# Feed-forward output product in pairs of column blocks, with seven block products for eight in 7 of 11 chunks

## The chip, the cores and the metric

The kernel runs on one core of a Trainium2 chip. The metric is the device time of one execution in microseconds (us). Before the change three executions took 1455.44, 1457.18 and 1457.25 us; the median is 1457.18 us.

The engines are named as in the profile: PE is TensorE (matrix products), PEld its weight load, DVE VectorE, ACT ScalarE, POOL GpSimd, SP SyncE, which issues the loads.

## The reference, cut to what matters

The layer takes `x` (256 tokens x 2048), runs two mixers with an output projection, adds the result to `x`, and then runs a gated feed-forward part:

```
h = rms_norm(x, norm_ffn)
gate_up = h @ w_ffn_in                    # (256 x 2048) @ (2048 x 11264)
ff_gate, ff_up = split(gate_up)           # each 256 x 5632
x = x + (silu(ff_gate) * ff_up) @ w_ffn_out    # (256 x 5632) @ (5632 x 2048)
```

Everything is float32. The change lies in the last line, the feed-forward output.

## The kernel before, in words

**Products.** All large products go through one function, `product` (L137). It makes 256 tokens times 512 columns of a weight. The tokens are two halves `m` of 128; the weight's rows are cut into k-tiles of 128, and four k-tiles by 512 columns are one chunk (1 MB). A float32 value is held as a high and a low part in the type float32r, and each block product is three matmuls: high x high (L152), high x low part of the weight (L153), low part of the activation x high (L154). A matmul takes a 128x128 piece of the activations as stationary operand and 512 columns of the weight as the moving one. So a chunk is 4 k-tiles x 2 halves x 3 = 24 matmuls. The feed-forward output has 11 chunks for each of 4 column blocks: 4 x 11 x 24 = 1056 matmuls, which accumulate into two PSUM banks per column block.

**Weights.** `fetch` (L112) loads a chunk on SP's queue into one of 4 buffers `raw`. `load_weights` (L121) cuts it in two halves of two k-tiles; for each, ACT writes the high part `whi` (a cast, L131) and DVE the low part `wlo` (raw minus high, L132), both 128x1024. There are 4 buffers of `whi` and 4 of `wlo`, so a cast has to wait until PE has finished with the half chunk four places earlier. A raw buffer is free when DVE has made the second low part from it.

**Activations.** In the feed-forward input (L646 on), every column block `j` of 512 hidden channels ends as `hn` (tokens x channels); PE transposes it in two pairs of k-tiles while the next products run, and ACT and DVE split it into `hT` high and low (L178, L179). These pieces are generators that move on by a step at every `tick`, half a chunk of products.

**Order.** A scheduler fixes the order of each engine's instructions at build time by priority; the preparation of weights has a priority some 500 instructions ahead of the products. On the chip every engine runs its own list in order and waits by semaphores.

**End.** After the 11 chunks of a column block DVE adds the two banks to the residual `xs` (L672) and SP stores them.

Of the kernel before, what the change touches and what calls it, by code (L numbers as in the profile page):

```python
# [10 lines left out]
F32 = mybir.dt.float32  # L11
# [6 lines left out]
P = 128  # L18
# [10 lines left out]
# columns of the packed per-partition parameters  # L29
# [4 lines left out]
N_WARM = 5  # L34


@with_exitstack
def block_kernel(ctx: ExitStack, tc: tile.TileContext, x, x_t, w_in, w_pa, w_pb, w_out, w_fi, w_fo,
# [11 lines left out]
    aux = ctx.enter_context(tc.tile_pool(name="aux", bufs=4, space=bass.MemoryType.PSUM))  # L50

# [21 lines left out]
    # ---------------------------------------------------------------- constants  # L73
# [7 lines left out]
    # products of zeros, so that TensorE's clock is up when the first weights are there  # L81
# [27 lines left out]
    # ---------------------------------------------------------------- weights  # L109
# [11 lines left out]
    def load_weights(w, nb, kc, n=2, raw=None):  # L121
        """One chunk of 4 k-tiles x 512 columns as high and low float32r halves."""
# [14 lines left out]
    def product(w, nb, n_chunks, act, prologue=None, last=False):  # L137
        """act^T (k x 256 tokens, high and low parts) times 512 columns of w."""
# [20 lines left out]

    def split_tiles(s):  # L160
# [12 lines left out]
    def transpose_split_pair(nat, pair, hi, lo, gain=None):  # L173
        """Transposed high and low parts of half of nat, times a gain per channel if given."""
        pt = transpose_pair(nat, pair)
        if gain is None:
# [4 lines left out]
            return  # L181
# [8 lines left out]
    def transpose_split(nat, hi, lo, gain=None, wait=2):  # L190
        for _ in range(wait):
            yield 1
        for pair in range(2):
            transpose_split_pair(nat, pair, hi, lo, gain)
            yield 1

# [6 lines left out]
    # ---------------------------------------------------------------- x: load, norm, transpose  # L203
# [18 lines left out]
    def x_block(c):  # L222
        """Loads of x^T and of the first weights in the order of their use, then of x itself."""
# [33 lines left out]
    # ---------------------------------------------------------------- constants of the mixers  # L257
# [6 lines left out]
    # lower bound: softmax over the two rows of logits, first row  # L264
# [21 lines left out]
    # ---------------------------------------------------------------- HGRN2, 4 heads at a time  # L286
# [15 lines left out]
    def hgrn_forget(ps, half, b, kk):  # L302
        """Cumulative log decay within 64 tokens, and k = 1 - f; [channel, head, token]."""
# [50 lines left out]
    def parts(L):  # L354
        """For each of the first three of 4 runs of L tokens: that run, columns of the later ones."""
# [57 lines left out]
    def next_factors(b, qT):  # L413
        """The queries as they are, then those of odd tokens decayed by one step."""
# [9 lines left out]
    def next_scores(kk, eq, acc):  # L424
        """Scores of each token with itself (zero elsewhere) and of odd tokens with the previous."""
# [67 lines left out]
    # ---------------------------------------------------------------- attention, 4 heads at a time  # L493
# [23 lines left out]
    def attention(half, pair, qT, kT, v, yh, yl):  # L517
# [3 lines left out]
        # a query of the first chunk of a tile does not see the tile's second chunk  # L521
# [96 lines left out]
    # ---------------------------------------------------------------- branch projections, merge  # L618
# [14 lines left out]
    # ---------------------------------------------------------------- output projection, residual  # L633
# [14 lines left out]
    # ---------------------------------------------------------------- SwiGLU  # L648
    act_x2 = picker(x2T)
    hT = []  # L650
    for j in range(NJ):
# [9 lines left out]
        start(transpose_split(hn, *hT[j]))  # L661
# [3 lines left out]
    for nb in range(4):  # L665
        ps = product(w_fo, nb, NJ, act_h, last=nb == 3)
        for m in range(2):
            pieces = 2 if nb == 3 and m == 1 else 1
            w = 512 // pieces
            for i in range(pieces):  # L670
                sl = slice(i * w, (i + 1) * w)
                nc.vector.tensor_tensor(out=xs[nb][:, m, sl], in0=ps[m][:, sl],  # L672
                                        in1=xs[nb][:, m, sl], op=ALU.add)
# [65 lines left out]
```

## Time and profile before

| | us |
|---|---|
| span of the profiled execution (first to last instruction) | 1454.8 |
| executions timed without a profile | 1455.44, 1457.18, 1457.25 |
| median of these, less the span | 2.4 |
| PE busy | 1446.9 (99%) |
| DVE busy | 805.1 (55%) |
| ACT busy | 685.9 (47%) |
| POOL busy | 36.5 (3%) |
| DMA engines, share of the span | 54.4% |

The profiled execution's own time is known by its span alone; the 2.4 us beside it are what lies around the span, and the spread of the executions. A matmul's row shows some 389 ns although the next one starts 0.227 us after it: matmuls are pipelined, so a sum over rows is not the time they take, and the start of the first and of the last have to be compared. "Idle before" in a row is the time for which the engine stood still before that group, with what ended it.

### The profile page before, as it was taken

What the parts mean: (1) busy time and instruction counts of PE and PEld (TensorE: products, weight loads), DVE (VectorE), ACT (ScalarE), POOL (GpSimd) and SP (SyncE); (2) the same over time, 40 slices, a digit from 0 to 9 for tenths busy, and PEclk for the clock granted to TensorE, in tenths of its full rate; (3) what the DMA queues carried; (4) which work ended last, traced back from release to release, by engine and by line L of the source; (5) the groups of instructions that cost most, each with busy time, mean ns of one, the idle gap of its engine ahead of it and who ended that gap; (6) DMA issues with size and microseconds to landing.
All of it is one profiled execution on the core that took longest, in us unless ns stands there. A gap on an engine that the chain in (4) does not pass through costs nothing.

```text
span 1454.8 us, 16455 instructions
## 1 busy us (share of the span) xinstructions
PE 1446.9 (99%) x6586; PEld 1201.6 (83%) x6586; DVE 805.1 (55%) x910; ACT 685.9 (47%) x869; POOL 36.5 (3%) x37
## 2 busy tenths in 40 slices
PE   8999999999999999999999999999999999999998
PEld 6888888888888888888888888888888888888887
DVE  6768868564554555655545555545554455444443
ACT  6756655555544444445444444444444444334332
POOL 0100100100000000100000000000000000000000
PEclk9999999999999999999999999999999999999999
DMA  9554354446555555555555555555555555655561
GB/s 361 211 201 163 129 191 155 173 156 215 183 203 198 207 193 183 194 182 178 198 178 199 177 199 185 191 184 192 187 189 198 179 197 179 207 199 204 199 208 52
DMA packets 42635, 275.68 MB, mean 189 GB/s; under 512 B 4800, under 2 KB 5056, under 8 KB 10816
## 3 DMA queue, kind: packets, MB, share of 16 engines
q1 hardware_dynamic: 42560, 274.64, 54.4%
q8 instruction: 51, 0.84, 0.2%
q14 instruction: 24, 0.20, 0.0%
HBM read 272.53 MB, written 2.10 MB: 189 GB/s over the span
## 4 chain that ended last, share of the span: by engine, by line
PE 99%; DMA 1%; SPq 0%; ACT 0%; issue 0%; DVE 0%; DVEq 0%
PE mm L152 31%; PE mm L153 31%; PE mm L154 31%; PE bank L169 2%; PE bank L400 1%; DMA xt<-in_x_t 1%; PE bank L430 0%; PE bank L476 0%; PE bank L527 0%; PE bank L555 0%; PE bank L565 0%; PE bank L474 0%; PE bank L567 0%; PE bank L463 0%; PE bank L563 0%; PE bank L529 0%
## 5 line engine op out<-in xcount | busy, mean ns | idle before, releaser
L132 DVE TENSOR_TENSOR wlo<-raw,whi 128x1024 fp32r<-128x1024 f32 (+1 forms) x508 | 618.6, 1220 | 595.0 <-ACT whi L131 594.8
L131 ACT CAST whi<-raw 128x1024 fp32r<-128x1024 f32 (+1 forms) x508 | 530.4, 1046 | 693.2 <-PE mm L154 670.8
L152 PE MATMUL mm<-whi,xTh 128*128 128x512 f32 x704 | 276.2, 397 | 2.8 <-ACT whi L131 2.8
L152 PE MATMUL mm<-whi,x2Th 128*128 128x512 f32 x704 | 276.3, 393 | 0.0
L154 PE MATMUL mm<-whi,xTl 128*128 128x512 f32 x704 | 274.9, 391 | 0.0
L153 PE MATMUL mm<-wlo,xTh 128*128 128x512 f32 x704 | 274.7, 390 | 0.0
L154 PE MATMUL mm<-whi,x2Tl 128*128 128x512 f32 x704 | 274.2, 390 | 0.0
L153 PE MATMUL mm<-wlo,x2Th 128*128 128x512 f32 x704 | 274.2, 389 | 0.0
L152 PEld LDWEIGHTS mm<-whi,xTh 128*128 128x128 f32 x704 | 132.1, 188 | 29.7 <-ACT whi L131 3.9
L154 PEld LDWEIGHTS mm<-whi,x2Tl 128*128 128x128 f32 x704 | 132.2, 188 | 28.1
L154 PEld LDWEIGHTS mm<-whi,xTl 128*128 128x128 f32 x704 | 132.2, 188 | 27.8
L153 PEld LDWEIGHTS mm<-wlo,x2Th 128*128 128x128 f32 x704 | 132.3, 188 | 26.9
L153 PEld LDWEIGHTS mm<-wlo,xTh 128*128 128x128 f32 x704 | 132.3, 188 | 26.7 <-DVE wlo L132 0.9
L152 PEld LDWEIGHTS mm<-whi,x2Th 128*128 128x128 f32 x704 | 132.2, 188 | 26.7
L152 PE MATMUL mm<-whi,hTh 128*128 128x512 f32 x352 | 137.2, 390 | 0.0
L153 PE MATMUL mm<-wlo,hTh 128*128 128x512 f32 x352 | 137.0, 389 | 0.0
L154 PE MATMUL mm<-whi,hTl 128*128 128x512 f32 x352 | 137.0, 389 | 0.0
L154 PEld LDWEIGHTS mm<-whi,hTl 128*128 128x128 f32 x352 | 66.1, 188 | 13.8
L152 PEld LDWEIGHTS mm<-whi,hTh 128*128 128x128 f32 x352 | 66.1, 188 | 13.8
L153 PEld LDWEIGHTS mm<-wlo,hTh 128*128 128x128 f32 x352 | 66.1, 188 | 13.5
L152 PE MATMUL mm<-whi,mTh 128*128 128x512 f32 x128 | 50.7, 396 | 0.0
L154 PE MATMUL mm<-whi,mTl 128*128 128x512 f32 x128 | 49.9, 390 | 0.0
(171 smaller groups left out, 947.0 us busy)
## 6 DMA issues: line engine op xcount, KB each, us to landing
raw<-in_w_fi SPq DMA_DIRECT2D x88, 1024.0 KB, 4.8
raw<-in_w_in SPq DMA_DIRECT2D x84, 1024.0 KB, 4.8
raw<-in_w_fo SPq DMA_DIRECT2D x44, 1024.0 KB, 4.7
raw<-in_w_out SPq DMA_DIRECT2D x16, 1024.0 KB, 4.8
raw<-in_w_pa SPq DMA_DIRECT2D x8, 1024.0 KB, 5.0
raw<-in_w_pb SPq DMA_DIRECT2D x8, 1024.0 KB, 4.8
raw<-in_w_in SPq DMA_DIRECT2D x8, 256.0 KB, 7.4
raw<-in_w_in SPq DMA_DIRECT2D x4, 512.0 KB, 8.3
```

What stands on the lines that cost most here:

```text
L131: nc.scalar.copy(hi[:, sl, :], src[:, sl, :])
L132: nc.vector.tensor_tensor(out=lo[:, sl, :], in0=src[:, sl, :], in1=hi[:, sl, :].bitcast(F32), op=ALU.subtract)
L152: nc.tensor.matmul(ps[m], lhsT=ah, rhs=wh, start=kc == 0 and k4 == 0, stop=False)
L153: nc.tensor.matmul(ps[m], lhsT=ah, rhs=wl, start=False, stop=False)
L154: nc.tensor.matmul(ps[m], lhsT=al, rhs=wh, start=False, stop=kc == n_chunks - 1 and k4 == 3)
L169: nc.tensor.transpose(out=pt[:, j, m * P:(m + 1) * P], in_=nat[:, m, c:c + P], identity=ident)
L400: nc.tensor.matmul(pl[:, j, :], lhsT=ek[:, g // 2, (g % 2) * P:(g % 2 + 1) * P], rhs=eq[:, g, :], start=True, stop=True)
```

## The change

The four column blocks of the feed-forward output are done as two pairs by a new function, `product_pair`. A pair's chunk has 4 k-tiles x 2 column blocks x 2 token halves = 16 block products, 48 matmuls, and needs two raw tiles (`r0`, `r1`, one per column block) and all four banks of one PSUM pool for its sums.

In the chunks 1, 2, 3, 5, 6, 7 and 9 the first two k-tiles are taken together as a 2x2 by 2x2 block product and done with seven products of sums (Winograd's form) instead of eight: 15 block products, 45 matmuls. It needs

- sums of the weights, made by `weight_forms` on DVE in each such chunk: four subtractions of 128x512 into `ta` and `tb`, which are then split into high and low like any weight. The weights of such a chunk are six tiles where a plain chunk has four; they are called here by the order in which they are made: **A** (k-tiles 0, 1 of block 0, products 1 and 2), **B** (`ta`, products 5 and 7), **C** (`tb`, products 6 and 4), **D** (k-tile 1 of block 1, 128x512, product 3), **E** and **F** (k-tiles 2, 3 of block 0 and of block 1). Still 4 buffers of `whi` and of `wlo` serve them in turn: E gets A's buffer, F gets B's, the next chunk's A, B, C, D get those of C, D, E, F;
- sums of the activations, made once per chunk by `act_forms` during the feed-forward input (one copy on ACT and four sums on DVE, all 128x128, and a split of 128x512), stored to DRAM from POOL's queue (512 KB each) and read back from POOL's queue, all seven in a row, into buffers of the feed-forward input's activations; the first two reads wait until the last column block of that input is through its first chunk, two for its second, two for its third, the last for its fourth;
- four more PSUM banks `ub` for the products 1, 5, 7, 6, which run through all seven chunks. They are the other pool's banks. After chunk 9 `sums` adds them into the residual: nine sums of 128x512 and a copy per pair.

```
+SEVEN = (1, 2, 3, 5, 6, 7, 9)
...
+    def halves(src):
+        n = src.shape[1]
+        hi = whi_p.tile([P, 2, 512], F32R, tag="hi", name=nm("whi"))
+        lo = wlo_p.tile([P, 2, 512], F32R, tag="lo", name=nm("wlo"))
+        split(hi[:, 0:n, :], lo[:, 0:n, :], src)
+        return [(hi[:, k, :], lo[:, k, :]) for k in range(n)]
+
+    def weight_forms(r0, r1):
+        ta = t6_p.tile([P, 2, 512], F32, tag="t6", name=nm("ta"))
+        tb = t6_p.tile([P, 2, 512], F32, tag="t6", name=nm("tb"))
+        b11, b21, b12, b22 = r0[:, 0, :], r0[:, 1, :], r1[:, 0, :], r1[:, 1, :]
+        sub = lambda out, x, y: nc.vector.tensor_tensor(out=out, in0=x, in1=y, op=ALU.subtract)
+        sub(ta[:, 0, :], b12, b11)
+        sub(ta[:, 1, :], b22, b12)
+        p1, p2 = halves(r0[:, 0:2, :])
+        p5, p7 = halves(ta)
+        sub(tb[:, 0, :], b22, ta[:, 0, :])
+        sub(tb[:, 1, :], b21, tb[:, 0, :])
+        p6, p4 = halves(tb)
+        p3, = halves(r1[:, 1:2, :])
+        return {1: p1, 2: p2, 3: p3, 4: p4, 5: p5, 6: p6, 7: p7}
+
+    def product_pair(w, nbs, n_chunks, act, forms, c_pool, u_pool, epilogue, last=False):
...
+                r = [fetch(w, nb, kc) for nb in nbs]
+                if kc in forms:
+                    tf = weight_forms(*r)
+                    ws = [[None, None] + halves(r[n][:, 2:4, :]) for n in range(2)]
+                else:
+                    ws = [halves(r[n][:, 0:2, :]) + halves(r[n][:, 2:4, :]) for n in range(2)]
...
+                for p in (1, 5, 7, 6, 2, 3, 4):
...
+                    if p in ub:
+                        triple(ub[p], a, tf[p], kc == seven[0], kc == seven[-1])
+                    else:
+                        triple(cb[dest[p]], a, tf[p], dest[p] not in begun, False)
...
+            if kc == seven[-1]:
+                epilogue(ub)
...
+    def act_forms(pt, keep):
+        s = t2([P, 4, P], "sf")
+        a11, a21, a12, a22 = (pt[:, k, m * P:(m + 1) * P] for k in range(2) for m in range(2))
+        op = lambda out, x, y, o: nc.vector.tensor_tensor(out=out, in0=x, in1=y, op=o)
+        nc.scalar.copy(s[:, 2, :], a21)
+        op(s[:, 0, :], a22, s[:, 2, :], ALU.add)
...
+        f = t6_p.tile([P, 2, 4, P], F32R, tag="t6", name=nm("sform"))
+        split(f[:, 0], f[:, 1], s)
+        nc.gpsimd.dma_start(out=keep, in_=f.bitcast(F32))
...
-    for nb in range(4):
-        ps = product(w_fo, nb, NJ, act_h, last=nb == 3)
...
+    for j in SEVEN:
+        forms[j] = t4([P, 2, 4, P], "sf", F32R)
+        nc.gpsimd.dma_start(out=forms[j].bitcast(F32), in_=kept[j])
+    for pair in range(2):
...
+        def sums(ub):
+            u2, u3 = t2([P, 512], "u2"), t2([P, 512], "u3")
+            add(x0[:, 0, :], x0[:, 0, :], ub[1])
+            nc.scalar.copy(u2, ub[1])
+            add(u2, ub[6], u2)
...
+        pools = (mm, aux) if pair == 0 else (aux, mm)
+        cb = product_pair(w_fo, nbs, NJ, act_h, forms, *pools, sums, last=pair == 1)
```

On PE, the list of before in the middle of a chunk of the feed-forward output (`mm` the two banks, `whi`, `wlo` the weight, `hT` the activations) is this:

```order
L153 MATMUL mm_1494_8742<-wlo_1534_8998,hTh_1344_7848 128x512
L154 MATMUL mm_1494_8742<-whi_1533_8997,hTl_1345_7849 128x512
L152 MATMUL mm_1493_8741<-whi_1533_8997,hTh_1344_7848 128x512
L153 MATMUL mm_1493_8741<-wlo_1534_8998,hTh_1344_7848 128x512
L154 MATMUL mm_1493_8741<-whi_1533_8997,hTl_1345_7849 128x512
```

and after the change, in chunk 6 of the first pair, from tile D to the first low part of E (`sf` the activation sums; `whi_1625` is D, `whi_1627` E, `whi_1629` F):

```order
L205 MATMUL mm_1523_8836<-whi_1625_9330,sf_1518_8828 128x512
L206 MATMUL mm_1523_8836<-wlo_1626_9331,sf_1518_8828 128x512
L207 MATMUL mm_1523_8836<-whi_1625_9330,sf_1518_8828 128x512
L205 MATMUL mm_1521_8834<-whi_1627_9334,hTh_1307_7597 128x512
L205 MATMUL mm_1522_8835<-whi_1627_9334,hTh_1307_7597 128x512
L205 MATMUL mm_1523_8836<-whi_1629_9338,hTh_1307_7597 128x512
L205 MATMUL mm_1524_8837<-whi_1629_9338,hTh_1307_7597 128x512
L206 MATMUL mm_1521_8834<-wlo_1628_9335,hTh_1307_7597 128x512
```

Where a block product's three matmuls stood together, the scheduler now puts the high parts of E and F ahead of E's low part. Counted through chunks 5 and 6 of a pair from chunk 5's first matmul, PE's list has the last use of chunk 5's B at 10, of A at 12, of C at 18, of D at 21; the highs of E at 22 and 23, those of F at 24 and 25, E's lows from 26 to 35, F's from 38 to 47; in chunk 6 the last use of A at 53, the highs of E at 67, its lows from 71.

On DVE, the list of before in the same part of the program is one low part after the other (two per raw tile):

```order
L132 TENSOR_TENSOR wlo_1623_9588<-raw_1621_9585,whi_1622_9587 128x1024
L132 TENSOR_TENSOR wlo_1625_9592<-raw_1621_9585,whi_1624_9591 128x1024
L132 TENSOR_TENSOR wlo_1628_9622<-raw_1626_9619,whi_1627_9621 128x1024
L132 TENSOR_TENSOR wlo_1630_9626<-raw_1626_9619,whi_1629_9625 128x1024
L132 TENSOR_TENSOR wlo_1633_9656<-raw_1631_9653,whi_1632_9655 128x1024
```

and after the change, from D of chunk 6 (`wlo_1626`) to A of chunk 7 (`raw_1631` and `raw_1632` are chunk 7's raw tiles, `wlo_1628` and `wlo_1630` are E and F of chunk 6):

```order
L166 TENSOR_TENSOR wlo_1626_9331<-raw_1616_9310,whi_1625_9330 128x512
L182 TENSOR_TENSOR ta_1633_9391<-raw_1632_9389,raw_1631_9387 128x512
L182 TENSOR_TENSOR ta_1633_9391<-raw_1632_9389 128x512
L182 TENSOR_TENSOR tb_1634_9392<-raw_1632_9389,ta_1633_9391 128x512
L166 TENSOR_TENSOR wlo_1628_9335<-raw_1615_9308,whi_1627_9334 128x1024
L182 TENSOR_TENSOR tb_1634_9392<-raw_1631_9387,tb_1634_9392 128x512
L166 TENSOR_TENSOR wlo_1630_9339<-raw_1616_9310,whi_1629_9338 128x1024
L166 TENSOR_TENSOR wlo_1636_9396<-raw_1631_9387,whi_1635_9395 128x1024
```

Three subtractions for the next chunk, which need its raw tiles, now stand ahead of the low part of E of the chunk that PE is at.

## Rows read from the trace of the kernel before

**Rows 1.** The page: its busy times, and its chain that ended last

```profile
PE 1446.9 (99%) x6586; PEld 1201.6 (83%) x6586; DVE 805.1 (55%) x910; ACT 685.9 (47%) x869; POOL 36.5 (3%) x37
...
PE 99%; DMA 1%; SPq 0%; ACT 0%; issue 0%; DVE 0%; DVEq 0%
```

**Rows 2.** Waits in 1205 to 1455 us: who waited for whom, us, times, longest

```profile
ACT whi L131 <- PE mm L154: 144.9, 87, 1.7
DVE wlo L132 <- ACT whi L131: 124.9, 87, 1.5
```

**Rows 3.** Timeline of PE: start, us, instruction; first and last of the feed-forward output, one transpose group

```profile
1210.37 0.39 PE L152 MATMUL mm<-whi,hTh 128*128 128x512 f32 x1
...
1218.53 0.60 PE L169 MATMUL bank<-ident,hn 128*128 128x128 f32 x4
1218.88 0.48 PE L152 MATMUL mm<-whi,hTh 128*128 128x512 f32 x1
...
1450.49 0.39 PE L154 MATMUL mm<-whi,hTl 128*128 128x512 f32 x1
```

**Rows 4.** Groups by line, 1210.3 to 1451 us: count, busy us, mean ns, idle before

```profile
L154 PE MATMUL mm<-whi,hTl 128*128 128x512 f32 x352 | 137.0, 389 | 0.0
...
L169 PE MATMUL bank<-ident,hn 128*128 128x128 f32 x8 | 1.2, 272 | 0.0
```

**Rows 5.** Busy times in 1213.8 to 1450.9 us: stretch, PE, PEld, DVE, ACT, POOL, clock, DMA

```profile
1213.80:1450.90 237.10, 237.08 (x1050) 195.96 (x1048) 108.42 (x93) 89.06 (x86) 0.00 (x0) 1.00 0.52 181
```

**Rows 6.** Groups of DVE and of ACT by shape, whole span: count, busy us, mean ns

```profile
L132 DVE TENSOR_TENSOR wlo<-raw,whi 128x1024 fp32r<-128x1024 f32 x500 | 613.3, 1228 | 592.7 <-ACT whi L131 592.6
L507 DVE TENSOR_TENSOR kb<-kb,rs 128x512 f32<-128x512 f32 x4 | 2.6, 684 | 0.0
...
L131 ACT CAST whi<-raw 128x1024 fp32r<-128x1024 f32 x500 | 525.8, 1053 | 690.6 <-PE mm L154 670.8 <-DVE wlo L132 6.6 <-ACT gate L615 4.6
L131 ACT CAST whi<-raw 128x512 fp32r<-128x512 f32 x8 | 4.6, 616 | 2.6 <-DMA raw<-in_w_in 2.6
```

**Rows 7.** Timeline of DVE, then of ACT: neighbours without idle time between them

```profile
14.57 2.50 DVE L132 TENSOR_TENSOR wlo<-raw,whi 128x512 fp32r<-128x512 f32 x4
...
22.69 2.35 DVE L132 TENSOR_TENSOR wlo<-raw,whi 128x1024 fp32r<-128x1024 f32 x2
...
76.93 1.05 ACT L131 CAST whi<-raw 128x1024 fp32r<-128x1024 f32 x1
77.88 0.68 ACT L299 ACTIVATE v<-mm,r 128x512 f32<-128x512 f32 x1
```

**Rows 8.** Timeline: a hand-over from PE to ACT to DVE, and one to PE

```profile
1052.13 0.39 PE L154 MATMUL mm<-whi,x2Tl 128*128 128x512 f32 x1
...
1052.55 1.05 ACT L131 CAST whi<-raw 128x1024 fp32r<-128x1024 f32 x1 [1.67 <-PE mm L154]
...
1053.64 1.23 DVE L132 TENSOR_TENSOR wlo<-raw,whi 128x1024 fp32r<-128x1024 f32 x1 [1.50 <-ACT whi L131]
...
7.65 0.69 DVE L132 TENSOR_TENSOR wlo<-raw,whi 128x512 fp32r<-128x512 f32 x1 [0.93 <-ACT whi L131]
...
8.39 0.50 PE L153 MATMUL mm<-wlo,xTh 128*128 128x512 f32 x1
```

**Rows 9.** DMA: loads of the feed-forward output, those of 0 to 60 us (KB, us to landing)

```profile
raw<-in_w_fo SPq DMA_DIRECT2D x44, 1024.0 KB, 4.7
...
raw<-in_w_in SPq DMA_DIRECT2D x10, 1024.0 KB, 9.7
...
x<-in_x SPq DMA_DIRECT2D x4, 512.0 KB, 12.2
```

**Rows 10.** DMA in 15 to 35 us, where loads queue: the mean rate

```profile
DMA packets 2335, 8.40 MB, mean 420 GB/s; under 512 B 202, under 2 KB 202, under 8 KB 1876
```

**Rows 11.** Timeline of DVE at the end: the last sum

```profile
1450.92 0.75 DVE L672 TENSOR_TENSOR x<-mm,x 128x256 f32<-128x256 f32 x2 [2.03 <-PE mm L154]
```

More of the change, by code (lines that the diff above doesn't have):

```diff
@@ new lines, in product_pair, with triple @@
+    def product_pair(w, nbs, n_chunks, act, forms, c_pool, u_pool, epilogue, last=False):
+        tag = {id(mm): "mm", id(aux): "bank"}
+        cb = {(m, n): c_pool.tile([P, 512], F32, tag=tag[id(c_pool)], name=nm("mm"))
+              for n in range(2) for m in range(2)}
+        ub = {}
+        count = [0]
+        def triple(ps, a, b, first, final):
+            (ah, al), (wh, wl) = a, b
+            nc.tensor.matmul(ps, lhsT=ah, rhs=wh, start=first, stop=False)
+            nc.tensor.matmul(ps, lhsT=ah, rhs=wl, start=False, stop=False)
+            nc.tensor.matmul(ps, lhsT=al, rhs=wh, start=False, stop=final)
+            count[0] += 1
+            if count[0] % 4 == 0:
+                tick()
+        begun = set()
+        seven = sorted(forms)
+        for kc in range(n_chunks):
+            end = kc == n_chunks - 1
+            with tc.high_priority(offset=min(PREP_AHEAD, tc.cur_priority - first_block[0])):
+                r = [fetch(w, nb, kc) for nb in nbs]
[4 more added lines that the diff above has]
+                    ws = [halves(r[n][:, 0:2, :]) + halves(r[n][:, 2:4, :]) for n in range(2)]
+            if kc in forms:
+                if not ub:
+                    ub.update({p: u_pool.tile([P, 512], F32, tag=tag[id(u_pool)], name=nm("mu"))
+                               for p in (1, 5, 7, 6)})
+                sf = forms[kc]
+                fo = {5: 0, 6: 1, 7: 2, 3: 3}
+                plain = {1: (0, 0), 2: (1, 0), 4: (1, 1)}
+                dest = {2: (0, 0), 3: (0, 1), 4: (1, 0)}
+                for p in (1, 5, 7, 6, 2, 3, 4):
+                    if p in fo:
+                        a = (sf[:, 0, fo[p], :], sf[:, 1, fo[p], :])
+                    else:
+                        k, m = plain[p]
+                        a = act(kc * 4 + k, m)
+                    if p in ub:
+                        triple(ub[p], a, tf[p], kc == seven[0], kc == seven[-1])
+                    else:
+                        triple(cb[dest[p]], a, tf[p], dest[p] not in begun, False)
+                        begun.add(dest[p])
+            ks = [k for k in range(4) if ws[0][k] is not None]
+            order = [(n, k, m) for n in range(2) for k in ks for m in range(2)]
+            if last and end:
+                order = [(n, k, m) for n in range(2) for m in range(2) for k in ks]
+            for n, k, m in order:
+                triple(cb[m, n], act(kc * 4 + k, m), ws[n][k], (m, n) not in begun,
+                       end and k == 3)
+                begun.add((m, n))
+            if kc == seven[-1]:
+                epilogue(ub)
+        return cb
@@ L660, in block_kernel, with add @@
         hT.append(split_tiles("hT"))
-        start(transpose_split(hn, *hT[j]))
+        if j in SEVEN:
+            kept[j] = dram.tile([P, 2, 4, P], F32, tag=f"kept{j}", name=nm("kept"))
+        start(transpose_split(hn, *hT[j], keep=kept.get(j)))
     act_h = picker(hT)
     out_v = out.rearrange("(m p) d -> p m d", p=P)
-    for nb in range(4):
-        ps = product(w_fo, nb, NJ, act_h, last=nb == 3)
[L667 to L673, printed above, removed]
-                nc.sync.dma_start(out=out_v[:, m, nb * 512 + i * w:nb * 512 + (i + 1) * w],
-                                  in_=xs[nb][:, m, sl])
+    forms = {}
+    for j in SEVEN:
+        forms[j] = t4([P, 2, 4, P], "sf", F32R)
+        nc.gpsimd.dma_start(out=forms[j].bitcast(F32), in_=kept[j])
+    for pair in range(2):
+        nbs = (2 * pair, 2 * pair + 1)
+        x0, x1 = (xs[nb] for nb in nbs)
+        def add(out, a, b):
+            nc.vector.tensor_tensor(out=out, in0=a, in1=b, op=ALU.add)
+        def sums(ub):
[3 more added lines that the diff above has]
+            add(u2, ub[6], u2)
+            add(u3, ub[7], u2)
+            add(x1[:, 0, :], x1[:, 0, :], u2)
+            add(x0[:, 1, :], x0[:, 1, :], u3)
+            add(x1[:, 1, :], x1[:, 1, :], u3)
+            for m in range(2):
+                add(x1[:, m, :], ub[5], x1[:, m, :])
+        pools = (mm, aux) if pair == 0 else (aux, mm)
+        cb = product_pair(w_fo, nbs, NJ, act_h, forms, *pools, sums, last=pair == 1)
+        for n, nb in enumerate(nbs):
+            for m in range(2):
+                pieces = 2 if nb == 3 and m == 1 else 1
+                w = 512 // pieces
+                for i in range(pieces):
+                    sl = slice(i * w, (i + 1) * w)
+                    add(xs[nb][:, m, sl], cb[m, n][:, sl], xs[nb][:, m, sl])
+                    nc.sync.dma_start(out=out_v[:, m, nb * 512 + i * w:nb * 512 + (i + 1) * w],
+                                      in_=xs[nb][:, m, sl])
     assert not running
```

16 lines of the change are left out of this document (13 added, 3 removed).

## The prediction

> **What bounds the kernel now.** I read the page's busy times first, then its chain that ended last. Both say PE: busy 99%, and 99% of the chain is PE [rows 1]. The waits in the feed-forward output say who waits for whom: ACT's casts wait for PE in all 87 cases and DVE's low parts wait for ACT [rows 2]. So weights are prepared as soon as PE gives a buffer back, and PE waits for nothing; its groups there have no idle time before them [rows 4]. In that stretch DVE is busy 108 of 237 us, ACT 89, the DMA engines 52%, and the granted clock is 1.00, the level of 2.4 GHz, throughout [rows 5]. A matmul less is therefore its whole pitch less, as long as the new work on DVE keeps pace.
>
> **The pitch.** The first matmul of the feed-forward output starts at 1210.37, the last at 1450.49 [rows 3]: 240.12 us for 1055 steps (1056 matmuls, 352 of each of three kinds [rows 4]) and two groups of four transposes at 0.35 us (1218.53 to 1218.88 [rows 3]). (240.12 - 0.7) / 1055 = 0.227 us. The 389 ns of a row is not the cost.
>
> **What goes.** 7 chunks x 2 pairs x one block product x 3 matmuls = 42 matmuls; PE's list falls from 1056 to 1014. 42 x 0.227 = 9.5 us. The order ahead of the feed-forward output is the same on PE, so nothing else goes.
>
> **What DVE and ACT get.** A plain pair chunk has four low parts of 128x1024, a chunk of seven has five, one of 128x512 and four subtractions of 128x512. Alone they last 1.23 and 0.68 us [rows 6], but neighbours overlap: two of 1024 span 2.35, so the second adds 1.13; four of 512 span 2.50, (2.50 - 0.69) / 3 = 0.60 [rows 7]. DVE: 5 x 1.13 + 5 x 0.60 = 8.7 us in a chunk that now lasts 45 x 0.227 = 10.2 us on PE (plain: 4.5 of 10.9). ACT: five casts at 0.95 (76.93 to 77.88 [rows 7]) and one of 0.62 [rows 6], 5.4 us. Both fit in sum; what decides is when a buffer comes free. So I walk two chunks of seven in a row, 5 and 6, time 0 at chunk 5's first matmul. A cast starts 0.42 after the start of the last matmul that used its buffer, that is 0.20 after the next matmul's place; a low part 0.03 after the cast's end; PE 0.05 after a low part's end [rows 8].
>
> Chunk 5, tile E takes A's buffer, used last by matmul 12: cast 2.72 + 0.20 = 2.92 to 3.97, low part 4.00 to 5.23. PE wants the highs at matmul 22 (21 x 0.227 = 4.77) and the low at 26 (5.67): 0.8 and 0.4 us to spare. F's cast follows at 3.87 and ends at 4.92, wanted at matmul 24 (5.22): 0.3 to spare. F's low part ends at 6.36, wanted at 38 (8.40).
>
> Chunk 6, the middle of a run of three, is tighter, since on DVE three subtractions for chunk 7 stand ahead of E's low part, and behind the first of them everything on DVE waits for chunk 7's raw tiles. Their two buffers come free at 5.23 and 6.36 (the low parts of E and F). A load alone takes 4.7 us [rows 9]: landed at 9.9 and 11.1. If the second one's bytes queue behind the first's at the 420 GB/s of [rows 10] (1.049 MB, 2.5 us), at 12.4. DVE itself gets there when D's low part is done; D takes F's buffer (matmul 47): 10.67 + 0.20 + 0.62 + 0.60 = 12.1. So the subtractions start at 12.1 to 12.4, take 3 x 0.60, and E's low part ends at 15.1 to 15.5. PE wants it at matmul 71 (15.89): 0.4 to 0.8 us to spare. Chunk 7 has no such subtractions ahead, and the chunks 4, 8 and 10 leave DVE half idle.
>
> In words: the cover of 5.6 us that a low part has before (three half chunks, 8.2 us, less 0.2 + 1.05 + 0.03 + 1.23) shrinks to some 0.3 to 0.8 us in the chunks of seven, but does not vanish. A late hand-over costs PE only what exceeds it. No row shows a hand-over on PE under such conditions. The bounds for the 14 chunks are nothing (PE is idle before none of the 1056 matmuls [rows 4], so there is none to win back either) and 14 x 0.7 = 10 us (E's low part ready one DVE operation of 1.13 late, less 0.4). I take 0.5 us in all, near the rows.
>
> The Trainium skill speaks against the raw loads: its page "DMA: Bandwidth & Descriptors", section "Bandwidth", puts the limit from HBM to one core at about 358 GB/s. By that I estimate the second raw tile's landing at 12.8 in place of 12.4 and the end of E's low part at 15.86, right where PE wants it: rival 2 below would be twice as likely as I make it. This trace disagrees: 420 GB/s over 20 us [rows 10].
>
> **Hidden parts.** In the feed-forward input DVE gets five operations and ACT two per block of seven; none with a 128x128 shape is in my rows, so I bound them above by 128x512: 5 x 0.68 = 3.4 us [rows 6], under the 5.6 us of cover there, once per 192 matmuls. Price with the cover gone: up to 7 x 3.4 = 24 us; I take nothing. The nine sums after chunk 9 (9 x 0.68 = 6.1) bring DVE to 8.7 + 4.5 + 6.1 = 19.3 us in the two chunks 9 and 10 that last 21.1 on PE, spare 1.8; the first of them waits for product 1 of chunk 9 (0.7 us into it) with D's low part behind it, which PE wants at 4.5. I take nothing, and 2 x 1.8 us as the other bound. The transfers from POOL's queue have no row at all. For a transfer of 512 KB the nearest rows are 4.7 us (1 MB alone) and 12.2 us (512 KB behind others) [rows 9]. The first read may start when the last block of the feed-forward input has done the first of its four chunks, three chunks of 24 x 0.227 = 5.45, so 16 us, before chunk 0 of the output. One after the other at 12.2 the seven land -4, 8, 20, 33, 45, 57, 69 us after chunk 0's start, and are wanted from about 11, 21, 31, 52, 62, 73, 94: hidden, by 11 us at the tightest (chunk 3). I take nothing; from (31 + 16) / 3 = 16 us per read the cover is gone.
>
> **The end** stays: the last sum in two pieces and its store, from 1450.92 to 1454.8 [rows 11].
>
> **Sum.** 1454.8 - 9.5 + 0.5 = 1445.8 us of span, and 2.4 us more in the median of the runs: 1448.2 us. Own range 1446 (lowest run 1455.4 less 9.5) to 1450.5.
>
> **Rivals.**
> 1. The saved matmuls turn into waits for E and F. The new buffer cycle has 0.3 to 0.4 us to spare where it had 5.6, and DVE runs its list in order; one operation ahead of E's low part at the wrong time and PE stands for 0.7 us in each of 14 chunks: 10 us, time about 1458, no change. Half of that gives 1453. For it: DVE is at 8.7 of 10.2 us. Against it: hand-overs in the rows are steady to 0.03 us.
> 2. The raw tiles come late, and the kernel gets slower. The middle chunk of each run (2 and 6 of each pair, four places) waits for a load that is issued only when chunk 5's F is split. It may take 12.85 - 6.36 = 6.5 us (15.89 less 1.23 and 1.8). Where loads queue they took 9.7 [rows 9]: then the subtractions start at 16.1, E's low part ends at 19.1, and PE waits 3.2 us; 4 x 3.2 = 13 us: 1457.2 - 9.5 + 13 = 1461. It decides against the change from 8.9 us per load (2.4 us each). Against it: here at most two loads are under way, and the engines are half idle. For it: the reads from POOL's queue come on top in the first run.
> 3. The reads of the activation sums come late. At 20 us each the last lands 7 x 20 - 16 = 124 us after chunk 0's start, 30 after PE wants it: 1478. Nothing but the lack of a row speaks for it.
> That the change does not remove the matmuls is excluded by PE's list.
>
> **Chances.** Forecast 0.62; rival 1 in part (1450.5 to 1454.2) 0.15, in full 0.11; rival 2 0.08; rival 3 0.04. A measurement of this kernel tells 0.2% (2.9 us) from no change, so faster means under 1454.3: 0.62 + 0.15 + 0.01 = 0.78; within 0.2%: rival 1 in full and mild cases of the others, 0.13; slower 0.09. Range 1446 to 1456, which leaves out the two slower cases and about half of the full rival 1, 0.18 in all.
>
> **What would show it.** In the new profile: 1014 matmuls with pitch 0.227 and no idle time before them; the feed-forward output from its first to its last matmul 230.6 us plus the stalls. Waits of PE for a low part of E (the tile `wlo` from L166) in every chunk of seven are rival 1; waits of DVE at L182 for a load, and of PE behind them, in chunks 2 and 6 alone are rival 2; PE waiting for `sf` is rival 3. DVE should be busy in the feed-forward output for some 108 + 14 x (5 x 1.23 + 5 x 0.68 - 4 x 1.23) + 12 = 185 of 231 us by its rows. A stretch with a clock under 1.00, or a feed-forward input that is longer than before, would make the prediction wrong in a way that no case above holds.

## The result

| | time, us | span of the profiled run | ratio to before |
|---|---|---|---|
| before | 1456.31 (1455.17 to 1457.25, 4 runs) | 1454.8 | |
| after | 1448.64 (1447.81 to 1451.2, 4 runs) | 1447.0 | 0.9947 [0.9933, 0.9961] |
| after, run once more | 1450.83 (1446.5 to 1454.2, 6 runs) | 1444.7 | 0.9960 [0.9945, 0.9975] |

The change makes the kernel faster by 0.5%. The forecast was 1448.2 us, the range 1446 to 1456. The next sections show that the gain came by the mechanism forecast, and that one term of the sum was too small by some 1 to 3 us. The profiled execution of the last row was the fastest of its six (1446.5 us), so its profile shows a mild case.

### The profile page after: what moved, and what is told of

Read it like the earlier page. It is cut to its first block, busy times and chain, and to the rows that moved or that the text cites. A ratio compares the mean times of both kernels' runs of the same rounds, so it can differ in the third digit from the quotient of the medians.

```text
span 1447.0 us, 16607 instructions
## 1 busy us (share of the span) xinstructions
PE 1439.2 (99%) x6544; PEld 1192.9 (82%) x6544; DVE 881.5 (61%) x1045; ACT 713.5 (49%) x913; POOL 44.2 (3%) x51
## 4 chain that ended last, share of the span: by engine, by line
PE 91%; DMA 4%; DVE 4%; issue 0%; ACT 0%; SPq 0%; DVEq 0%; ACTq 0%
PE mm L157 26%; PE mm L156 26%; PE mm L158 26%; DMA raw<-in_w_fo 4%; PE mm L206 3%; PE mm L207 2%; PE mm L205 2%; DVE wlo L166 2%; PE bank L263 2%; PE bank L510 1%; DVE ta L182 1%; DVE tb L182 1%; PE mu L205 0%; PE mu L207 0%; PE mu L206 0%
## 5 line engine op out<-in xcount | busy, mean ns | idle before, releaser
L136 DVE TENSOR_TENSOR wlo<-raw,whi 128x1024 fp32r<-128x1024 f32 (+1 forms) x420 | 510.7, 1219 | 453.2 <-ACT whi L135 452.9
L135 ACT CAST whi<-raw 128x1024 fp32r<-128x1024 f32 (+1 forms) x420 | 438.2, 1045 | 529.7 <-PE mm L158 499.7
L165 ACT CAST whi<-raw 128x1024 fp32r<-128x1024 f32 x88 | 84.3, 985 | 80.4 <-PE mm L207 62.0
L166 DVE TENSOR_TENSOR wlo<-raw,whi 128x1024 fp32r<-128x1024 f32 x88 | 97.9, 1137 | 23.5 <-ACT whi L165 23.0
L206 PE MATMUL mm<-wlo,hTh 128*128 128x512 f32 x268 | 104.9, 391 | 1.6 <-DVE wlo L166 1.6
L207 PE MATMUL mm<-whi,hTl 128*128 128x512 f32 x268 | 104.4, 389 | 0.0
L205 PE MATMUL mm<-whi,hTh 128*128 128x512 f32 x268 | 95.1, 390 | 0.0
L206 PEld LDWEIGHTS mm<-wlo,hTh 128*128 128x128 f32 x268 | 50.3, 188 | 13.7 <-DVE wlo L166 3.3
L205 PEld LDWEIGHTS mm<-whi,hTh 128*128 128x128 f32 x268 | 50.2, 188 | 10.5
L207 PEld LDWEIGHTS mm<-whi,hTl 128*128 128x128 f32 x268 | 50.3, 188 | 10.3
```

The costliest lines, as they stand in the source:

```text
L135: nc.scalar.copy(hi[:, sl, :], src[:, sl, :])
L136: nc.vector.tensor_tensor(out=lo[:, sl, :], in0=src[:, sl, :], in1=hi[:, sl, :].bitcast(F32), op=ALU.subtract)
L165: nc.scalar.copy(hi, src)
L166: nc.vector.tensor_tensor(out=lo, in0=src, in1=hi.bitcast(F32), op=ALU.subtract)
L205: nc.tensor.matmul(ps, lhsT=ah, rhs=wh, start=first, stop=False)
L206: nc.tensor.matmul(ps, lhsT=ah, rhs=wl, start=False, stop=False)
```

## The profile after

The page of the changed kernel, busy times and the chain that ended last, beside [rows 1]:

```profile
PE 1439.2 (99%) x6544; PEld 1192.9 (82%) x6544; DVE 881.5 (61%) x1045; ACT 713.5 (49%) x913; POOL 44.2 (3%) x51
...
PE 91%; DMA 4%; DVE 4%; issue 0%; ACT 0%; SPq 0%; DVEq 0%; ACTq 0%
```

PE has 42 matmuls fewer (6586 to 6544) and is still the bound, but the chain now runs through DMA and DVE for 8%, where it was PE for 99%. Somewhere PE waits. Its timeline in the feed-forward output shows where; the first and the last row answer to [rows 3]:

```profile
1208.81 0.39 PE L205 MATMUL mm<-whi,hTh 128*128 128x512 f32 x1
...
1236.02 1.07 PE L205 MATMUL mm<-whi,hTh 128*128 128x512 f32 x4
1237.67 0.50 PE L206 MATMUL mm<-wlo,hTh 128*128 128x512 f32 x1 [0.58 <-DVE wlo L166]
1238.00 0.39 PE L207 MATMUL mm<-whi,hTl 128*128 128x512 f32 x1
...
1442.62 0.39 PE L207 MATMUL mm<-whi,hTl 128*128 128x512 f32 x1
```

From first to last it is 233.81 us. Four matmuls from 1236.02 should be over at 1236.93; the next one, the first that reads the low part of E in chunk 2, starts at 1237.67, 0.74 late. The same place is late by 0.62 us in chunk 6, and in the second pair by 0.70 and 0.20; the matmul behind each adds 0.1. That is 2.7 us in four places, the middle chunks (2 and 6 of each pair, which stand between two other seven-product chunks), and nowhere else more than 0.13 us.

What the waits of the stage name (who waited for whom, us, times, longest), where [rows 2] had ACT behind PE and DVE behind ACT alone:

```profile
DVE ta L182 <- DMA raw<-in_w_fo: 26.4, 14, 3.2
...
PEld mm L206 <- DVE wlo L166: 3.5, 5, 1.0
```

And DVE and SP around chunk 2, where the wait is made. First SP's two loads of the next chunk's raw tiles, then DVE from D's low part to E's:

```profile
1226.03 0.33 SPq L120 DMA_DIRECT2D raw<-in_w_fo  x1
1227.16 0.33 SPq L120 DMA_DIRECT2D raw<-in_w_fo  x1
```

```profile
1232.57 0.69 DVE L166 TENSOR_TENSOR wlo<-raw,whi 128x512 fp32r<-128x512 f32 x1 [1.52 <-ACT whi L165]
1234.58 0.69 DVE L182 TENSOR_TENSOR ta<-raw,raw 128x512 f32<-128x512 f32 x1 [1.32 <-DMA raw<-in_w_fo]
1235.19 0.68 DVE L182 TENSOR_TENSOR ta<-raw 128x512 f32<-128x512 f32 x1
1235.79 0.68 DVE L182 TENSOR_TENSOR tb<-raw,ta 128x512 f32<-128x512 f32 x1
1236.39 1.22 DVE L166 TENSOR_TENSOR wlo<-raw,whi 128x1024 fp32r<-128x1024 f32 x1
```

DVE is done with D's low part at 1233.3 and stands for 1.32 us until the second raw tile is there, 7.4 us after its issue. E's low part, last row, is behind the three subtractions and ends at 1237.6, where PE waits for it. The DMA engines over the same stretch (40 slices of 0.3 us from 1225):

```profile
GB/s 0 0 0 0 0 0 218 164 27 273 382 410 382 437 410 410 382 382 328 382 382 437 437 410 382 164 82 55 55 27 0 0 0 0 0 0 0 0 0 0
DMA packets 289, 2.11 MB, mean 175 GB/s; under 512 B 32, under 2 KB 32, under 8 KB 32
```

Bytes flow from 1226.8, at some 400 GB/s to 1232.5, and then a tail at 164 down to 27 GB/s goes on to 1234. The subtraction starts 0.6 us behind it.

## Experiments

Theory T: the gain is 42 matmuls at 0.227 us; the price is paid in the four middle chunks alone, where E's low part stands on DVE behind subtractions that wait for the next raw tile. Rivals were that the pairing itself gives or takes time (P), that each seven-product chunk pays for the hand-over of E and F wherever it stands (H), that the three subtractions have no room however early the tiles land (D), and that the activation sums cost time (S). "Stage" is from the start of the first to the start of the last matmul of the feed-forward output; 42 matmuls less and nothing else would be 240.12 - 9.53 = 230.59 us.

| run | time, us | ratio to before | stage, us |
|---|---|---|---|
| pairs | 1456.62 (1455.65 to 1457.72) | 0.9998 [0.9989, 1.0007] | 240.12 |
| isolated | 1449.75 (1448.05 to 1451.02) | 0.9950 [0.9938, 0.9963] | 233.35 |
| long | 1454.17 (1452.67 to 1458.24) | 0.9985 [0.9976, 0.9994] | 237.94 |
| e_first | 1447.30 (1446.33 to 1447.37) | 0.9932 [0.9920, 0.9944] | 230.63 |
| halves | 1450.26 (1449.26 to 1450.71) | 0.9954 [0.9941, 0.9966] | 234.00 |
| no_forms | 1449.16 (1447.51 to 1449.45) | 0.9945 [0.9932, 0.9957] | 232.37 |
| interleaved | 1459.84 (1457.26 to 1462.12) | 1.0020 [1.0011, 1.0028] | 242.99 |
| again (the changed kernel) | 1450.83 (1446.5 to 1454.2) | 0.9960 [0.9945, 0.9975] | 232.14 |
| nine | 1443.61 (1443.05 to 1444.94) | 0.9911 [0.9897, 0.9925] | 228.33 |
| nine_halves | 1443.28 (1442.61 to 1445.49) | 0.9912 [0.9897, 0.9928] | 228.28 |

### pairs

```
-SEVEN = (1, 2, 3, 5, 6, 7, 9)
+SEVEN = ()
...
```

> The column blocks are paired as in the changed kernel, but no chunk uses sums: all eleven go as eight products per two k-tiles, and no activation sums are made or kept (the table of seven-product chunks is empty). Theory T (the gain is the 42 matmuls that are gone, at 0.227 us each, less stalls in the four chunks that stand between two seven-product chunks): 1056 matmuls in the stage again and no stall, so the stage takes 239.6 to 240.3 us as before the change and the time is that of before, 1455.5 to 1457 us. Rival P (the pairing itself, with four accumulators filled side by side, gives or takes part of the time): the stage differs from 240.1 us by more than 1 us either way.

The stage is 240.12 us, to the last digit that of [rows 3], and the time that of before. P is out: the order in pairs costs and gives nothing.

### isolated

```
+SEVEN = (1, 3, 5, 7, 9)
```

> Seven products in chunks 1, 3, 5, 7 and 9 alone: five in each pair of column blocks instead of seven, and none stands behind another. Theory T: 30 matmuls fewer than before, 6.8 us; no seven-product chunk is followed by another, so that no subtraction that waits for a load stands ahead of the low part of E, and PE never waits: stage 233.3 us, about 0.5 us shorter than with seven such chunks (233.8), time 1448 to 1449.8 us. Rival H (each seven-product chunk costs its own wait for E or F at the hand-over of buffers, 2.7 us over 14 chunks, 0.2 each): stage 240.1 - 6.8 + 10 x 0.2 = 235.3 us, time 1450 to 1452 us.

Stage 233.35 us, time 1449.75: T to 0.1 us. 30 matmuls less are 240.12 - 6.81 = 233.31. Where no seven-product chunk is followed by another, PE waits for no low part, so ten hand-overs of E and F cost nothing, and H is out. The changed kernel has twelve matmuls fewer than this one and a longer stage (233.81).

### long

```
+SEVEN = (1, 2, 3, 4, 5, 6, 7)
```

> Seven products in chunks 1 to 7: the same 14 chunks and the same 42 matmuls fewer as in the changed kernel, but in one run of seven in each pair instead of runs of three, three and one. Theory T: five chunks of each pair stand between two others instead of two, ten in all instead of four. At 0.68 us each (2.7 us over four) the stalls are 6.8 us; where the lateness is carried on from chunk to chunk (from the issue of the second load to its landing 7.3 us, three subtractions 1.9, the low parts of E and F 2.4: 11.6 us for a chunk that takes PE 10.2) each after the first is 1.4 us and they are 12.6 us. So the stage takes 237.5 to 243.5 us (233.8 before), and the time is 1452 to 1459 us. Rival H (a cost of each seven-product chunk, wherever it stands): the stage and the time are as with the changed kernel, 233.8 and 1448.6 us.

The same 42 matmuls fewer, and a stage 4.1 us longer than that of the changed kernel (233.81). PE waits before the low part of E in exactly the ten middle chunks; the last of the first run is the worst. PE, then DVE:

```profile
1279.60 1.07 PE L205 MATMUL mm<-whi,hTh 128*128 128x512 f32 x4
1282.05 0.50 PE L206 MATMUL mm<-wlo,hTh 128*128 128x512 f32 x1 [1.38 <-DVE wlo L166]
```

```profile
1279.56 0.69 DVE L182 TENSOR_TENSOR ta<-raw,raw 128x512 f32<-128x512 f32 x1 [2.22 <-DMA raw<-in_w_fo]
1280.17 0.69 DVE L182 TENSOR_TENSOR ta<-raw 128x512 f32<-128x512 f32 x1
1280.77 1.22 DVE L166 TENSOR_TENSOR wlo<-raw,whi 128x1024 fp32r<-128x1024 f32 x1
```

The ten gaps are 0.12 to 1.54 us, 5.9 in sum, and 1.1 for the matmuls behind them; the stage is 7.35 over 230.59. The lower of T's two sums (6.8) was near; lateness is not carried on at 1.4 us a chunk. A likely reason, not tested, is that a late PE also asks later for the next tile.

### e_first

```
-        sub(ta[:, 0, :], b12, b11)
-        sub(ta[:, 1, :], b22, b12)
+        for early in (sub(ta[:, 0, :], b12, b11), sub(ta[:, 1, :], b22, b12)):
+            if low_of_e[0] is not None:
+                tc.add_manual_dep(early.ins, low_of_e[0].ins.name, ...)
...
```

> As the changed kernel, but on DVE the low part of E stands ahead of the next chunk's two subtractions that make ta, everywhere. Theory T: the wait of DVE for the second raw tile stays, but no longer stands ahead of E's low part; the four gaps of PE, 2.7 us, go; the stage takes 231.0 to 231.3 us and the time is 1445.5 to 1446.5 us. If F's low part, which stays behind the two subtractions, were late in its place, the gaps would stand twelve matmuls later in the same four chunks. Rival H (the hand-over of buffers, or DVE's load in such a chunk): the gaps stay, 1448.6 us.

All four gaps are gone: the stage is 230.63 us, 42 pitches less than before and 0.04. No time is spent by PE on a low part. DVE in chunk 2 (the pair in the first row is D's and E's low part), beside the rows of the changed kernel above:

```profile
1235.03 1.88 DVE L166 TENSOR_TENSOR wlo<-raw,whi 128x512 fp32r<-128x512 f32 x2
1236.83 0.68 DVE L186 TENSOR_TENSOR ta<-raw,raw 128x512 f32<-128x512 f32 x1
1237.43 0.69 DVE L186 TENSOR_TENSOR ta<-raw 128x512 f32<-128x512 f32 x1
1238.04 1.22 DVE L166 TENSOR_TENSOR wlo<-raw,whi 128x1024 fp32r<-128x1024 f32 x1
```

The waits of the stage now have this row, where the changed kernel had 26.4 us in 14:

```profile
DVE ta L186 <- DMA raw<-in_w_fo: 3.2, 2, 1.7
```

One part of T was wrong: I had the wait for the tile stay behind E's low part. It goes, because DVE comes to the subtractions later and the tile has landed by then. The stage is 0.4 us under the 231.0 to 231.3 that I gave, the time 0.8 us above the 1445.5 to 1446.5.

### halves and interleaved

```
-                r = [fetch(w, nb, kc) for nb in nbs]
+                r = [wraw_p.tile([P, 4, 512], F32, tag="raw", name=nm("raw")) for _ in nbs]
+                for k in (0, 2):
+                    for raw, nb in zip(r, nbs):
+                        nc.sync.dma_start(out=raw[:, k:k + 2, :], in_=w[nb, kc, :, k:k + 2, :])
```

> As the changed kernel, but each pair of raw weight tiles is loaded as four transfers of 512 KB in place of two of 1 MB: k-tiles 0 and 1 of both column blocks first, then k-tiles 2 and 3 of both. The three subtractions stay ahead of the low part of E on DVE (the scheduler now puts D's low part behind them too); they read k-tiles 0 and 1 alone, which land earlier, by up to half of the 8.4 us that the pair took. Theory T (the stalls come from the landing of the pair, for which these subtractions wait): DVE's waits for the load, 26.4 us over 14 in the changed kernel, fall by half at least, the gaps of PE go with nothing moved on DVE in E's favour; stage 230.6 to 231.2 us between its first and last matmul (233.8 in the changed kernel, 230.6 with E's low part first), time 1446 to 1447.5 us. Rival D (it is the 1.9 us of subtractions themselves that E's low part has no room for, however early the tiles land): the four gaps stay, 0.5 us or more each, 1448 us or more.

A miss for T as I had built it: DVE's waits for the load fall from 26.4 to 20.9 us only, and the four gaps stay (0.6 to 0.7 us; in chunk 2 of the first pair 0.48 us of it come where PE first reads D's low part, the rest at E's). The run is no clean test, since on DVE D's low part and the fourth subtraction now stand ahead of E's low part too. The scheduler had issued both halves of the first block ahead of the second's, and what moves is slower. The DMA engines from 1225, in slices of 0.3 us, to be held against the changed kernel's above:

```profile
GB/s 0 0 0 0 0 82 191 259 273 287 273 259 246 355 314 410 382 273 218 232 246 232 369 382 410 410 369 260 137 68 55 0 0 0 0 0 0 0 0 0
DMA packets 576, 2.10 MB, mean 175 GB/s; under 512 B 64, under 2 KB 64, under 8 KB 576
```

The same 2.1 MB go in twice the packets, now all under 8 KB, at 190 to 410 GB/s where most went at 380 to 437, and end no earlier after the first issue (1225.79). The Trainium skill, page "DMA: Bandwidth & Descriptors", section "Bandwidth", has the rule to batch transfers to 1 MiB or more for at least three quarters of the peak (its figures are for GpSimd's queue); the two rates here agree with it.

The second build held the order of the four transfers as meant (`tc.keep_in_program_order` around each), and DVE's order in the middle chunks as in the changed kernel.

> The run with halved loads again, now with the order of the four transfers held as it was meant: k-tiles 0 and 1 of the first block, then of the second, then k-tiles 2 and 3 of both (the scheduler had put both halves of the first block ahead of the second's, so that the second block's first half was third on the queue and landed 6.2 us after its issue). On DVE the two subtractions into ta stand behind D's low part and, in the four middle chunks, the three subtractions ahead of E's low part, as in the changed kernel. Theory T (the gaps come from the landing of the second raw tile): its first half lands some 2 us earlier or more, DVE finds it there, the low part of E ends 0.6 us ahead of its use, and the four gaps go with DVE's order as it was: stage 230.6 to 231.2 us, 1446 to 1447.7 us. Rival D (the three subtractions, 1.9 us, have no room there however early the tiles land): gaps of 0.2 us or more in the four chunks, 1448 us or more.

T is wrong again in its numbers, and D, which has a gap in all four places, too. In the first pair chunk 6 has no gap and chunk 2 has one of 1.17 us; in the second, chunk 2 has 0.43 and chunk 6 none. From its issue to the first subtraction the second block's first half took 7.4 us in chunk 2 (1229.63 to 1237.02) and 6.3 in chunk 6; it landed 7.0 and 5.5 us from its issue in the second pair. A whole tile had landed in 6.4 to 7.4 us in the changed kernel's four places; here two transfers are queued behind the half. So splitting brings the first half in hardly earlier. The kernel is slow for another reason: held in program order, the loads of the second pair stand on SP's queue behind the stores of the first pair's sums, and PE stands at the seam of the pairs (SP's timeline, then PE's):

```profile
1323.55 6.00 SPq L833 DMA_DIRECT2D out<-x  x4
1329.64 15.36 SPq L238 DMA_DIRECT2D raw<-in_w_fo  x12
```

```profile
1328.07 0.39 PE L225 MATMUL mm<-whi,hTl 128*128 128x512 f32 x1
1336.23 1.22 PE L223 MATMUL mm<-whi,hTh 128*128 128x512 f32 x2 [7.77 <-ACT whi L165]
```

The wait costs more than its length: behind it the granted clock is 0.50, the level of 1.2 GHz, and until 1340.2 PE's matmuls start 0.43 us apart or more, where they had 0.227 (stretch, PE, PEld, DVE, ACT, POOL, clock, DMA, GB/s):

```profile
1336.00:1340.00 4.00, 3.73 (x8) 2.55 (x9) 1.23 (x1) 1.06 (x2) 0.00 (x0) 0.50 1.00 394
```

Splitting did not bring the landing that T asked for, so neither run is the test it was meant as. The next two decide between T and D, by chance.

### no_forms and again

```
-                        a = (sf[:, 0, fo[p], :], sf[:, 1, fo[p], :])
+                        a = act(kc * 4 + fo[p] // 2, fo[p] % 2)
...
```

> As the changed kernel, but the activation sums are left out of the computation: nothing of them is made in the feed-forward input stage, written to DRAM or read back, and the products that use a sum use a plain activation tile in its place. The matmuls, the weights and their loads are as before. Theory T (that work lies wholly beside PE's): stage 233.5 to 234.1 us with the same four gaps, 3 us of them in sum, time within 1 us of the changed kernel's, 1447.6 to 1449.6 us. Rival S (the sums cost time in the input stage by DVE, ScalarE or PSUM, or their seven reads slow the first weight loads): the time is lower by 1 to 4 us, and it is lower ahead of the stage or in the first run of chunks 1 to 3 alone.

> The changed kernel itself once more, beside the others on one chip: how far the gaps of the four middle chunks differ from one execution to another, against which the 1.3 us of them without sums (3.0 us with them) is to be read. Theory T (the gaps are set by when loads land, which differs): they sum to anything from 1 to 3.5 us, stage 232 to 234 us, 1448 to 1449.5 us. Rival S (the sums and their reads cause the difference): 2.7 us or more again, and above all in chunk 2 of the first pair, where the reads have just ended.

Without the sums the stage is 232.37 us, 1.8 over 230.59, against 3.2 in the first profile of the changed kernel and under the 233.5 that T had at least. That looked like rival S, until the changed kernel, profiled again with its sums, gave 232.14, within T's range (its median time, 1450.83, is above T's 1449.5). The gaps differ from one execution to another, and the eight middle chunks of the two executions, with the four of no_forms, say by what. From the issue of the second load to the start of the first subtraction, and the gap before E's low part, us:

| execution | pair 0, chunk 2 | chunk 6 | pair 1, chunk 2 | chunk 6 |
|---|---|---|---|---|
| after | 7.42, gap 0.74 | 7.36, gap 0.62 | 7.49, gap 0.70 | 6.46, gap 0.20 |
| again | 7.07, gap 0.45 | 6.38, gap 0 | 6.26, gap 0.10 | 7.23, gap 0.38 |
| no_forms | 6.88, gap 0.03 | 7.25, gap 0.60 | 6.99, gap 0.19 | 7.14, gap 0.31 |

Over 7.2 us every gap is 0.38 or more; at the four of 6.9 or less it is 0.2 at most. In all twelve E's low part ends 3.03 us after the start of the first subtraction, and the gap is the time by which that end comes after PE asks for the tile, and some 0.05 us more. The place without a gap, chunk 6 of again, where DVE stands 0.13 us for the tile (from 1274.39 to 1274.52): SP's issue of the second load, then DVE, then PE:

```profile
1268.14 0.33 SPq L120 DMA_DIRECT2D raw<-in_w_fo  x1
```

```profile
1273.70 0.69 DVE L166 TENSOR_TENSOR wlo<-raw,whi 128x512 fp32r<-128x512 f32 x1 [1.07 <-ACT whi L165]
1274.52 0.69 DVE L182 TENSOR_TENSOR ta<-raw,raw 128x512 f32<-128x512 f32 x1
1275.13 0.68 DVE L182 TENSOR_TENSOR ta<-raw 128x512 f32<-128x512 f32 x1
1275.73 0.69 DVE L182 TENSOR_TENSOR tb<-raw,ta 128x512 f32<-128x512 f32 x1
1276.34 1.22 DVE L166 TENSOR_TENSOR wlo<-raw,whi 128x1024 fp32r<-128x1024 f32 x1
```

```profile
1277.15 1.07 PE L205 MATMUL mm<-whi,hTh 128*128 128x512 f32 x4
1278.06 0.39 PE L206 MATMUL mm<-wlo,hTh 128*128 128x512 f32 x1
```

and the DMA engines of that stretch, 40 slices of 0.3 us from 1267, to be held against chunk 2 of the first profile. The first four slices carry about the same (0.2 MB); then the bulk goes in 14 slices at a mean of 427 GB/s, in place of 15 at 397, and the tail is three slices in place of five:

```profile
GB/s 0 0 0 355 82 109 109 382 410 437 437 410 437 437 437 437 410 437 437 437 437 300 55 55 0 0 0 0 0 0 0 0 0 0 0 0 0 0 246 137
```

This is what the split loads were to show: the same program, the same three subtractions ahead of E, an earlier landing, no gap. There E's low part ends at 1277.56, 0.5 us before PE asks for it (last row of PE's timeline, without a wait), so D is out. Of S nothing is seen: the stage with its sums was the shorter one, and the input stage takes 489.62 us with and without them. A cost under the 1.7 us by which the changed kernel's two profiles differ is not excluded. What makes one transfer slower than its like is not shown.

### nine and nine_halves

```
-SEVEN = (1, 2, 3, 5, 6, 7, 9)
+SEVEN = (1, 2, 3, 4, 5, 6, 7, 8, 9)
...
+    slots = [t4([P, 2, 4, P], "sf", F32R) for _ in range(7)]
...
+            if kc in SEVEN:
+                load_form(sf)
```

> Seven products in chunks 1 to 9 of each pair, 54 matmuls fewer than before in place of 42, with the low part of E ahead of the next chunk's ta as in the run with E first. The nine tiles of sums go through seven buffers: each is loaded again when its chunk is done, 18 reads in all on POOL's queue. Theory T: the low part of F, then the load of the next tile into the same buffer (7.3 us at most from its issue), two subtractions 1.3 and F's low part 1.2 come to 9.8 us for a chunk that takes PE 10.2, so that no lateness builds up; stage 240.1 - 54 x 0.227 = 227.9 us, time 2.7 us under that of E first, 1444 to 1445.2 us. Rival L (over eight chunks in a row the loads fall behind all the same): gaps in the later chunks of each run, growing along it, 0.5 us or more each for some ten chunks; 1447 to 1455 us.

> As the run with nine such chunks, with each pair of raw tiles loaded as four transfers of 512 KB, k-tiles 0 and 1 of both first. Theory T: there is no gap left to remove, the time is that of nine, 1444 to 1445.2 us. Rival L (late loads in the long run): here the first halves land early enough, and this is faster than nine by what its gaps were, 1444 to 1445.5 us.

With E's low part first, nine such chunks in a row run without late loads: the stage is 228.33 us (227.87 by 54 pitches), the largest single gap 0.11 us, and the time 1443.6 us, 0.9% under before and some 5 us under the changed kernel. The stage is 0.4 us over the forecast of 227.9, the time 0.4 us under the 1444 to 1445.2. It is the best version here; halved loads add nothing (1443.3).

## Why the prediction was right, and where its sum was off

**PE as the bound, the pitch, 42 matmuls.** Right. Three runs give the pitch again: e_first -9.49 us for 42, isolated -6.77 for 30, pairs 0 for none. The stretch of the changed kernel, beside [rows 5] (stretch, PE, PEld, DVE, ACT, POOL, clock, DMA, GB/s):

```profile
1208.80:1443.00 234.20, 232.59 (x1023) 190.44 (x1021) 176.25 (x197) 111.84 (x117) 0.53 (x1) 1.00 0.52 189
```

The clock is 1.00, the level of 2.4 GHz, as before. DVE is busy 176 us where I said 185: neighbours overlap more than durations taken alone show.

**The walk of chunks 5 and 6.** The structure was right: the only late places are those it named, and E's hand-over in the other ten chunks holds. Set beside chunk 6 of the first pair (time 0 = 1263.4), D's low part is done at 12.2 (forecast 12.1) and the loads are issued at 4.9 and 6.1 (5.2 and 6.4). Then the step that failed: the pair of loads. I took 4.7 us for one alone and 2.5 more for the bytes of the second at 420 GB/s, 7.2 us from the first issue; it took 8.5 there (1268.32 to 1276.81), so the subtractions started at 13.4, not 12.4, and E's low part ended at 16.4 in place of 15.5, with PE asking at 15.9. The first load took 4.6 to 5.0 us in the twelve places, about the 4.7 that I had. The second landed 2.4 to 3.6 us behind it, 3.1 or more in nine of the twelve, where I had 2.5. Here are the two loads of this chunk, then those of chunk 6 of again (us to landing in the last column):

```profile
raw<-in_w_fo SPq DMA_DIRECT2D x1, 1024.0 KB, 5.0
raw<-in_w_fo SPq DMA_DIRECT2D x1, 1024.0 KB, 7.2
```

```profile
raw<-in_w_fo SPq DMA_DIRECT2D x1, 1024.0 KB, 5.0
raw<-in_w_fo SPq DMA_DIRECT2D x1, 1024.0 KB, 6.3
```

The 420 GB/s of [rows 10] come near the middle of a transfer (397 and 427 above); what I left out is that the middle can run slower and ends in a tail, and that both vary. The load was allowed 6.5 us from its second issue; the table above puts the start of the gaps at 6.3 to 6.9.

**The 0.5 us for hand-overs.** This is the term that was mis-sized: the stage lost 3.2 us in the first profile and 1.55 in the second. Its range (0 to 10 us) held that.

**Rivals.** 1 is out (isolated, e_first). 2 was the one at work, in its mild form: 0.2 to 0.7 us per place, not the 3.2 us of a load of 9.7. Its threshold, 8.9 us for a load, was not reached. I had put it at 0.08 only as a rival that makes the kernel slower; its mild form had no term but the 0.5 us. 3 is out: PE never waits for `sf`, whose reads take

```profile
sf<-kept POOLq DMA_DIRECT2D x7, 512.0 KB, 6.1
```

**Hidden work.** Right. The feed-forward input takes 489.62 us from its first matmul to the output's first, before and after. First the row of before, then that of after; the ends are the first rows of [rows 3] and of PE's timeline above:

```profile
720.75 0.39 PE L152 MATMUL mm<-whi,x2Th 128*128 128x512 f32 x1
```

```profile
719.19 0.39 PE L156 MATMUL mm<-whi,x2Th 128*128 128x512 f32 x1
```

The sums after chunk 9 cost nothing either: isolated has them, and its stage is within 0.04 us of what its matmuls take. My bound for a 128x128 operation was 0.68 us; 21 of the 28 are in this row (mean in ns), at less than half of it:

```profile
L297 DVE TENSOR_TENSOR sf<-bank,sf 128x128 f32<-128x128 f32 x21 | 6.1, 292 | 2.8 <-ACT sf L298 2.3
```

**The sum.** The nearness of 1448.2 to 1448.64 is partly luck. Of the span's 7.8 us, 6.3 are the stage; 1.56 lie ahead of the feed-forward input (the two rows above), in work that the change does not touch. That start came between 718.6 and 721.4 us in the twelve profiles, without any order by kernel. And the 2.4 us that I added to the span were 1.6 here (1448.64 less 1447.0). The two made up for most of the 2.7 us that the stage lost beyond my 0.5.

**The rule of the Trainium skill.** The prediction set the 358 GB/s of the Trainium skill (page "DMA: Bandwidth & Descriptors", section "Bandwidth") against the trace. By that figure the landing was later (12.8) and rival 2 likelier, which came out nearer to what happened; but most slices of the two transfers above run at 382 to 437 GB/s, which contradicts the rate itself for this one core, and of the 0.9 us by which the late transfer shown is longer than the early one, 0.6 are its tail.

## What to carry to other kernels

Ask of each wait in an engine's in-order list what stands behind it: a low part that was ready to go stood behind three subtractions for the next chunk, and ordering it ahead of them gave back all that the wait cost, and nine such chunks in a row then ran without a late load. When the spare time of a step is smaller than the scatter of the transfer it rests on, take the transfer's ends from rows and expect a loss, not the mean rate. And compare a stage by its own first and last instruction, since the start ahead of it moved by up to 2.8 us between these profiles with nothing changed there.

## What the runs showed of the hardware that was not expected

- Two loads of 1 MB on one queue, issued 1.1 to 1.4 us apart: the second was read 6.3 to 7.5 us after its own issue, in otherwise equal places of one kernel. The bytes ran at up to 437 GB/s; the last of them at 27 to 82 GB/s for 1.2 us in one place, at 55 for 0.6 us in another.
- A transfer of 512 KB with one ahead of it and two more queued behind it landed 5.5 to 7.3 us from its issue in four places (interleaved), where the second load of 1 MB, with none behind, took 6.4 to 7.4 (after).
- After PE had stood for 7.77 us, the granted clock was 0.50 in the next 4 us, and matmuls that had started 0.227 us apart started 0.43 us apart or more (interleaved).
- The changed kernel scattered by 3.4 us over four runs and by 7.7 over six, e_first by 1.0 over five. That late loads make the scatter is not shown: isolated, whose PE waits for none, scattered by 3.0 over five.
